# Mixing part of a two-layer encoder: decay chain and 16-block inverse on VectorE, rotary beside the root, two merges ahead of the last gate

## The chip, the cores and the metric

The kernel runs on one core of one Trainium2 chip. A core has five engines that follow their own instruction lists and wait for one another by semaphores: TensorE (PE, matmuls), VectorE (DVE), ScalarE (ACT), GpSimd (POOL) and SyncE (SP, which here only issues DMAs). The metric is device time in microseconds (us) of one execution of the whole program. An instruction list is executed in its order: an instruction that waits holds up everything behind it on its engine.

## The reference

`x` has 256 tokens of 1024 channels. After a first LayerNorm come two equal layers. Each is a mixing part and an expert part, each with a residual and a LayerNorm:

```python
p = h @ w_in            # 5648 columns, split by meaning:
ya = _global_gqa(aq, ak, av, ...)          # A: 8 query heads, 2 key heads, RMSNorm + rotary on q and k
yb = _neighbourhood_attn(bq, bk, bv, rpb)  # B: 4 heads, a window on the token grid
yc = _gdn_bidir(cq, ck, cv, cz, cbf, cbb, caf, cab, ...)  # C: gated delta rule, both directions
ga, gb, gc = sigmoid(gate logits)
mix = ga * (ya @ wa) + gb * (yb @ wb) + gc * (yc @ wc)
return mix @ w_out
```

Branch C is the long one. Its log decay is `g = -exp(A_log) * softplus(a + dt_bias)`; a five-tap convolution with SiLU makes q, k and v; q and k are scaled to unit length; and for each chunk of 64 tokens (4 chunks, 4 heads, 2 directions) a unit lower triangular 64 x 64 system is solved:

```python
decay = exp(where(incl, gc[..., :, None] - gc[..., None, :], -inf))   # gc: running sum of g
m   = where(strict, einsum('nbhid,nbhjd->nbhij', k_beta, kc) * decay, 0.0)
sol = triangular_solve(m + eye(C), rhs, lower=True, unit_diagonal=True)
```

The expert part routes each token to 2 of 32 SwiGLU experts; the weights of all 32 are read in each layer.

## The kernel before

Everything is kept in float32; the projections are made as three products of a high and a low part (`mm3`). Weights come in units of 128 x 1024 numbers. For each unit SP issues one DMA (`w_...`), ACT makes the high part (`uh_...`, a cast) and DVE the low part (`ul_...`, a subtraction, L190). The table `POOL` names the units whose low part POOL makes. The units stand in rings of four, so a DMA, a cast or a subtraction can only go ahead as far as products before it have been done.

TensorE's order is written out: `projections` goes through `ORDER`, the list of projections (`ga0`: first half of branch A's gate, `cqk`, `cz`, `cv`: branch C, `akv`, `aq`: branch A, `bqk`, `bv`: branch B, and the other gates), then `merge` multiplies each branch's result by its matrix (tiles `y0a...`, `y0b...`, `y0c...` in layer 0), `turn_mix` transposes the sum (`tpm`), and `project` does `w_out`, the residual, the LayerNorm and the router. Between two product groups `pump` may let a side line take its next step: `key_line`, `query_line` (rotary of branch A), `delta_line` (branch C), `attention_line` and `router_line` are generators, and the table `LAGS` says how long after one step the next is due, on a clock that `mm` counts up from the sizes of the matmuls. So `LAGS` sets where in TensorE's list a side line's matmuls stand. On the other engines a scheduler orders the instructions by readiness and by priority (`high_priority`), but `issue_after` and `manual_schedule` can pin them.

Names in what follows, in the order in which they occur in a layer:

- `conv(i, b)`: the convolution, ten multiplies-and-adds on DVE for each of three pieces (piece 2 is v, bank `cv`), a tanh on ACT and one more DVE instruction. `norm_rope`: RMS (square on ACT, reduce and scale on DVE, power -1/2 on POOL, L243, in `rsqrt`), then normalise (DVE), rotary (two POOL multiplies, one DVE multiply, one DVE addition). `k` gives `kTA`, `q` gives `qA`, transposed to `qTA`.
- `delta_line`, decay: softplus by a short series, some 20 instructions on DVE in the tiles `gap` and `sb` (16 columns each), ending with `g`. Then `eb` (sums of g by matmul), `R` (three POOL multiplies, 128 x 512), `db` (three products of R with masks), their exponentials `E` on ACT.
- `delta_line`, unit length: transposes `qk`, squares, reduce, `rsqrt`, then `kh` and two `qd` for each token half (placeA, placeF), transposed to `kT` and `qdT`; `gr` is the gram of k with k and q; sixteen DVE multiplies put the decay on it, which gives `Z`.
- `delta_line`, inverse: the 16 x 16 diagonal blocks of Z are picked (`Zc`), sent through memory to another layout (`d1`, `Zd`), inverted by 30 small instructions (L165, 15 to 64 columns), sent back (`d2`, `Wc`), spread into `X` and `Y` (placeF), and TensorE's `T16`, `X16`, `Y16`, `T32` build the 64 x 64 inverses from them.
- `PLACES` tells which tiles share a stretch of memory (placeA ... placeX); when a place is free, the first weights of the expert part are fetched into it.

All tiles of both layers have the layer's number in their names; the rows of the profile leave buffer numbers out. The functions that the change touches, with the line numbers of the profile:

Of the kernel before, what the change touches and what calls it, by code (L numbers as in the profile page):

```python
# [10 lines left out]
F32 = mybir.dt.float32  # L11
# [4 lines left out]
OP = mybir.AluOpType  # L16
# [29 lines left out]
POOL = (1, 2, 5, 13, 14, 15, 17, 18, 21, 23, 50, 62)  # L46
LAGS = {
    "delta": [15.03, 1.23, 3.7, 10.0, 0, 0.76, 53.51, 0, 0, 0.8, 0.24, 0.0, 0.52, 1.67, 1.37, 0, 2.87, 2.23, 0, 2.03, 1.99, 0, 2.87, 1.99, 0, 2.87, 6.3],
    "key": [10.0],
    "query": [16.22, 1.92, 1.92],  # L50
    "attention": [0, 6.46, 2, 0, 6.46, 1.24, 0, 6.46, 2, 0, 6.91, 2, 0, 6.46, 2, 0, 6.46, 2],
    "router": [7.35],
}
ORDER = ("ga0", "cqk", "cz", "cv", "akv", "aq", "ga1", "bqk", "bv", "gb0", "gb1", "gc0", "gc1")
# [63 lines left out]
def kernel(ctx: ExitStack, tc: tile.TileContext, a: dict, out: bass.AP):  # L118
# [24 lines left out]
    def st(shape, tag, name, bufs=1, dt=F32, side="left"):  # L143
# [134 lines left out]
    def stream(srcs, first, beside):  # L278
# [11 lines left out]
        def cut():  # L290
# [27 lines left out]
    def mixer(l, fetch, norm):  # L318
# [41 lines left out]
        for n in ORDER:  # L360
            if n[0] == "g":
                want(n, 2576 + "abc".index(n[1]) * 1024 + int(n[2]) * 512, 512)
            else:
                want(n, *COLS[n])
        NK = {"a": 4, "b": 2, "c": 2}
        for br in "abc":
            wv = a[f"w_branch_{br}"][l].rearrange("(k p) f -> p k f", p=128)
            w = 1024 // NK[br]
            for u in range(NK[br]):
                srcs.append((wv[:, :, u * w:(u + 1) * w], f"br{l}{br}{u}"))  # L370
        wo = a["w_out"][l]
# [180 lines left out]
        cs = [of(f"cs{i}", 2, S) for i in range(3)]  # L552

        def conv(i, b):
# [15 lines left out]
        def norm_rope(b, t, n, which, dst, name):  # L570
# [3 lines left out]
            xv = x8(x[:, :n * 64])  # L574
            raw = x8(b) if which else xv
            if not which:
                A.copy(x[:, :n * 64], b)
            sq = y
            A.activation(sq[:, :n * 64], b if which else x[:, :n * 64], AF.Square)
            rs = of(f"rs{t}", 8)  # L580
            V.tensor_reduce(out=rs[:, :n], in_=x8(sq[:, :n * 64]), axis=AX.X, op=OP.add)
            rsqrt(rs[:, :n], rs[:, :n], 1.0 / 64.0, 1e-6, n)
            tt(V, xv, raw, rs[:, :n, None].to_broadcast([128, n, 64]), OP.mult)
            yv = x8(y[:, :n * 64])
            s5 = gc_[:, which, 1, t].rearrange("p (a b e) -> p a b e", a=2, b=2)
            for b_ in range(2):
# [38 lines left out]
        def delta_line(vbank, zb):  # L625

            szg = of("szg", 2, 256)
            ba = of("ba", 2, 2, 2, 4)
            for t in range(2):
                V.tensor_copy(ba[:, :, :, t], zb[t][:, 256:272].rearrange("p (a d h) -> p a d h", a=2, d=2))  # L630
                A.activation(szg[:, t], zb[t][:, :256], AF.Tanh, scale=0.5)
                stt(szg[:, t], szg[:, t], 1.0, zb[t][:, :256], OP.add, OP.mult)
            tt(G, szg.rearrange("p t (h d) -> p (t h) d", d=64), szg.rearrange("p t (h d) -> p (t h) d", d=64),
               gn[:, 2:3].to_broadcast([128, 8, 64]), OP.mult)
            beta = of("beta", 2, 8)
            A.activation(beta, ba[:, 0].rearrange("p d t h -> p d (t h)"), AF.Tanh, scale=0.5)
# [1031 lines left out]
```

## Time and profile before

| | us |
|---|---|
| median of three runs | 1435.94 |
| lowest, highest | 1431.05, 1437.71 |
| the profiled execution | 1434.16 |
| its span, first to last instruction | 1432.4 |
| mixing part, layer 0 | about 0 to 270 |
| expert part, layer 0 | about 270 to 715 |
| mixing part, layer 1 | about 715 to 975 |
| expert part, layer 1 | about 975 to 1432 |

The limits between the parts are read from the timeline of TensorE. The profile shows one execution. A row of a timeline is one or several equal instructions in succession; "[3.64 <-DVE gap L169]" at its end says that the engine had stood idle 3.64 us before it and which instruction ended that. "PEclk 0.50" in a table of windows is TensorE's granted clock: 1.00 is 2.4 GHz, 0.50 is 1.2 GHz, and a value between them is a window with both.

### The profile page before, as it was taken

How to read it: one execution, taken by the hardware profiler on the slowest of the kernel's cores; microseconds unless marked ns; L12 is line 12 of the kernel's file. 1: busy time of each engine (PE TensorE's matmuls, PEld its weight loads, DVE VectorE, ACT ScalarE, POOL GpSimd, SP SyncE). 2: the span in 40 equal slices, each digit the busy share in tenths (PEclk: the TensorE clock that was granted, in tenths of full speed). 3: DMA queues.
4: the chain of work that ended last, by engine and by line, in shares of the span. 5: the costliest groups of instructions: out<-in, count | busy, mean ns of one | idle time of the engine just before them, and what ended most of it. 6: DMA issues, size and time to landing. Idle time of an engine off the chain costs nothing. (4 is left out here: it accounts for less than half of the span.)

```text
span 1432.4 us, 23895 instructions
## 1 busy us (share of the span) xinstructions
PE 1348.6 (94%) x9778; PEld 893.5 (62%) x9778; DVE 614.0 (43%) x1221; ACT 400.2 (28%) x761; POOL 258.6 (18%) x327
## 2 busy tenths in 40 slices
PE   8889999899998999999889999999999899999986
PEld 7877777655555555555377877875555555555632
DVE  6887567522231222222269866774222122222214
ACT  4445543211121111211144465332111111111111
POOL 4474303300000000000036661132000000000000
PEclk9989999999999999999999999999999999999998
DMA  7735769799999999999846366798999999999994
GB/s 231 213 107 145 245 243 347 303 408 418 419 418 414 419 419 418 419 418 420 350 142 205 122 194 223 269 354 314 420 419 419 418 419 418 418 419 419 418 419 194
DMA packets 114533, 479.88 MB, mean 335 GB/s; under 512 B 25169, under 2 KB 38001, under 8 KB 65521
## 3 DMA queue, kind: packets, MB, share of 16 engines
q1 hardware_dynamic: 112464, 471.85, 84.3%
q0 software_dynamic: 1376, 5.24, 1.0%
q8 instruction: 80, 1.31, 0.4%
q10 hardware_dynamic: 576, 1.18, 0.2%
q14 instruction: 37, 0.30, 0.1%
HBM read 476.40 MB, written 1.84 MB: 334 GB/s over the span
## 5 line engine op out<-in xcount | busy, mean ns | idle before, releaser
L180 PE MATMUL h<-w,h 128*64 128x256 f32 x2016 | 232.2, 387 | 21.8 <-PEq L1413 11.1
L180 PEld LDWEIGHTS h<-w,h 128*64 128x64 f32 x2016 | 144.0, 139 | 101.0 <-issue 16.9
L174 DVE SCALAR_TENSOR_TENSOR hid<-gate,h 128x256 f32<-128x256 f32 x64 | 26.9, 421 | 404.9 <-ACT gate L1504 404.9
L174 DVE SCALAR_TENSOR_TENSOR op<-mo,rt,op 64x512 fp32r<-64x512 f32 x128 | 96.0, 750 | 221.1 <-ACT op L1535 220.2
L1535 ACT ACTIVATE op<-mo,rt 64x512 fp32r<-64x512 f32 x128 | 87.4, 683 | 310.6 <-PE mo L180 271.2
L180 PE MATMUL mo<-w,hidT 128*64 128x512 f32 x720 | 168.1, 595 | 3.5 <-DMA w<-in_w_dram 2.0
L165 POOL TENSOR_TENSOR W<-P,rt 128x128 f32<-128x128 f32 x64 | 24.3, 400 | 774.8 <-PE PT L186 700.3
L1504 ACT ACTIVATE gate<-h 128x256 f32<-128x256 f32 x64 | 24.6, 384 | 405.9 <-PE h L180 405.9
L180 PEld LDWEIGHTS mo<-w,hidT 128*64 128x64 f32 x720 | 51.3, 137 | 92.3 <-issue 80.8
L180 PE MATMUL h<-w,xg 128*64 128x256 f32 x864 | 96.9, 380 | 2.4 <-ACT h L1478 2.4
L180 PE MATMUL h<-wl,h 128*64 128x256 f32 x768 | 86.3, 381 | 2.2 <-ACT h L1478 1.5
L180 PEld LDWEIGHTS h<-w,xg 128*64 128x64 f32 x864 | 61.0, 137 | 34.3 <-ACT h L1478 3.9
L180 PEld LDWEIGHTS h<-wl,h 128*64 128x64 f32 x768 | 53.9, 137 | 30.6 <-ACT h L1478 2.4
L180 PE MATMUL mo<-wl,hidT 128*64 128x512 f32 x304 | 69.8, 596 | 0.9 <-DMA wl<-in_w_dram 0.9
L180 PE MATMUL my<-op,PT 128*128 128x512 f32 x256 | 69.3, 410 | 0.8 <-DVE op L174 0.6
L180 PEld LDWEIGHTS my<-op,PT 128*128 128x128 f32 x256 | 45.4, 188 | 23.9 <-issue 13.2
L180 PE MATMUL xg<-P,hh 128*128 128x256 f32 x256 | 54.8, 294 | 0.3 <-DVE P L165 0.3
L180 PEld LDWEIGHTS xg<-P,hh 128*128 128x128 f32 x256 | 39.1, 188 | 24.8 <-issue 24.6
L180 PE MATMUL h<-wl,xg 128*64 128x256 f32 x416 | 48.3, 382 | 5.1 <-DMA wl<-in_w_dram 3.4
L180 PE MATMUL xg<-P,hl 128*128 128x256 f32 x256 | 51.0, 281 | 0.0
L180 PEld LDWEIGHTS mo<-wl,hidT 128*64 128x64 f32 x304 | 20.7, 137 | 35.5 <-issue 30.7
L180 PEld LDWEIGHTS h<-wl,xg 128*64 128x64 f32 x416 | 28.6, 137 | 22.5 <-DMA wl<-in_w_dram 6.5
(459 smaller groups left out, 2455.7 us busy)
## 6 DMA issues: line engine op xcount, KB each, us to landing
w<-in_w_dram SPq DMA_DIRECT2D x268, 1024.0 KB, 19.9
wl<-in_w_dram SPq DMA_DIRECT2D x112, 1024.0 KB, 19.9
w_gb<-in_w_in_dram SPq DMA_DIRECT2D x16, 512.0 KB, 3.6
w_gc<-in_w_in_dram SPq DMA_DIRECT2D x16, 512.0 KB, 4.6
w_wo<-in_w_out_dram SPq DMA_DIRECT2D x16, 512.0 KB, 4.4
w_ga<-in_w_in_dram SPq DMA_DIRECT2D x14, 512.0 KB, 5.4
w_cqk<-in_w_in_dram SPq DMA_DIRECT2D x8, 512.0 KB, 3.4
w_aq<-in_w_in_dram SPq DMA_DIRECT2D x8, 512.0 KB, 4.3
```

The costliest lines, as they stand in the source:

```text
L165: return eng.tensor_tensor(out=o, in0=x, in1=y, op=op).ins
L174: return V.scalar_tensor_tensor(out=o, in0=x, scalar=s, in1=y, op0=op0, op1=op1)
L180: ins = T.matmul(o, l, r, start=start, stop=stop, skip_group_check=True).ins
L1504: A.activation(g, b[:, :256], AF.Tanh, scale=0.5)
L1535: A.activation(hi, src, AF.Copy, scale=w)
```

## The change

What it does, piece by piece:

1. Decay: the series keeps its small tiles in a PSUM bank, takes fewer instructions (factors are folded into `scalar_tensor_tensor`), has -exp(A_log) made by POOL, and the convolution of v is placed behind it (`issue_after(decayed)`).
2. The convolution's first multiply is on ACT instead of DVE. The exponentials of `eb` are made twice, one copy in PSUM.
3. `norm_rope`: the rotary works on the raw values, beside the root; the normalisation comes last. The scale-and-add ahead of the power moves from DVE to POOL there and for the unit length of k and q.
4. `kh`, `qd`, the masks `Em` and the betas come in another order: transposes of v first, masks (all four now on DVE), a step of the side line, then `kh` and `qd`, pinned behind the last low part (`issue_after(scope["cut"])`). `cs[0]` lies where `kq` needs it, so the POOL copy L763 goes.
5. Blocks: `Zc` is made by one multiply and three multiply-adds; the 30 instructions of the inverse move from POOL to DVE; `X` is spread by four ACT copies, `Y` by one DVE multiply, instead of sixteen POOL multiplies.
6. `ORDER` has the merges of branches a and b ahead of `gc1`, c behind it. The gated sums of b and c stand in PSUM, and all additions to `mix` are on DVE.
7. The softmax normalisation moves from DVE to ACT; `LAGS`, `POOL` and `PLACES` have other entries.

The core of the diff:

```diff
-POOL = (1, 2, 5, 13, 14, 15, 17, 18, 21, 23, 50, 62)
+POOL = (1, 2, 5, 13, 14, 15, 17, 18, 21, 23, 56, 62)
 LAGS = {
-    "delta": [15.03, 1.23, 3.7, 10.0, 0, 0.76, 53.51, 0, ...
+    "delta": [15.03, 1.23, 3.7, 4.5, 5.5, 0, 0.76, 12.0, 20.0, 0, ...
-ORDER = ("ga0", "cqk", "cz", "cv", "akv", "aq", "ga1", "bqk", "bv", "gb0", "gb1", "gc0", "gc1")
+ORDER = ("ga0", "cqk", "cz", "cv", "akv", "aq", "ga1", "bqk", "bv", "gb0", "gb1", "gc0", "a", "b", "gc1", "c")
...
-    def rsqrt(o, x, scale, eps, n):
+    def rsqrt(o, x, scale, eps, n, eng=V):
         with tc.high_priority(offset=PRI):
-            ts(V, o, x, scale, OP.mult, eps, OP.add)
+            ts(eng, o, x, scale, OP.mult, eps, OP.add)
             return G.tensor_tensor(out=o, in0=o, in1=mhalf[:, :n], op=OP.pow)
...
             for m in range(2):                      # conv
-                ts(V, y[:, m], bv[:, m], cw[:, ch, 2:3], OP.mult)
+                A.activation(y[:, m], bv[:, m], AF.Copy, scale=cw[:, ch, 2:3])
...
-            rsqrt(rs[:, :n], rs[:, :n], 1.0 / 64.0, 1e-6, n)      # norm_rope
-            tt(V, xv, raw, rs[:, :n, None].to_broadcast([128, n, 64]), OP.mult)
+            rsqrt(rs[:, :n], rs[:, :n], 1.0 / 64.0, 1e-6, n, G)
...
             tt(V, xv, xv, gc_[:, which, 0, t:t + 1].to_broadcast([128, n, 64]), OP.mult)
-            tt(V, dst, xv, yv, OP.add)
+            tt(V, xv, xv, yv, OP.add)
+            tt(V, dst, xv, rs[:, :n, None].to_broadcast([128, n, 64]), OP.mult)
...
+            for c2 in range(2):                     # delta_line
+                decayed = stt(sc[:, c2], acc, C("half")[:, c2:c2 + 1], nea, OP.mult, OP.mult).ins
...
-            conv(2, vbank)
+            with tc.issue_after(decayed):
+                conv(2, vbank)
...
+            with tc.issue_after(scope["cut"]):
+                for t, b in enumerate(tokens):
+                    tt(V, x4(kh[:, t]), x4(b[:, 256:512]), bc(rk[:, t, 4:8]), OP.mult)
...
-                tt(G, tv, Zd[:, j + 1:, j:j + 1].to_broadcast([128, n, m]),
-                   W0[:, j:j + 1, :m].to_broadcast([128, n, m]), OP.mult)
-                tt(G, W0[:, j + 1:, :m], W0[:, j + 1:, :m], tv, OP.subtract)
+                    tt(V, tv, Zd[:, j + 1:, j:j + 1].to_broadcast([128, n, m]),
+                       W0[:, j:j + 1, :m].to_broadcast([128, n, m]), OP.mult)
+                    tt(V, W0[:, j + 1:, :m], W0[:, j + 1:, :m], tv, OP.subtract)
...
-            for w, o in ((1, Y), (0, X)):
-                for x0 in (0, 8):
-                    for b_ in range(4):
-                        tt(G, o[:, x0:x0 + 8, b_ * 16:b_ * 16 + 16], Wc[:, w, x0:x0 + 8],
-                           bm[:, b_:b_ + 1].to_broadcast([128, 8, 16]), OP.mult)
+            for b_ in range(4):
+                A.activation(X[:, :, b_ * 16:b_ * 16 + 16], Wc[:, 0], AF.Copy, scale=bm[:, b_, 0:1])
+            tt(V, Y.rearrange("p x (b j) -> p x b j", b=4), Wc[:, 1][:, :, None, :].to_broadcast([128, 16, 4, 16]),
+               bm[:, None].to_broadcast([128, 16, 4, 16]), OP.mult)
...
-                    stt(x, x, 1.0, b, OP.add, OP.mult)            # merge
-                    if br != "a":
-                        tt(G if br == "b" or t else V, mix[:, t, sl], mix[:, t, sl], x, OP.add)
+                    if br == "a":
+                        stt(x, x, 1.0, b, OP.add, OP.mult)
+                    else:
+                        with tc.high_priority(offset=PRI):
+                            stt(b, x, 1.0, b, OP.add, OP.mult)
+                            tt(V, mix[:, t, sl], mix[:, t, sl], b, OP.add)
```

How it moves instructions, at three places. First ACT in layer 0, where the exponentials of `eb` and `db` stand. Before:

```order
L190 CAST uh_ga101_787<-w_ga101_749 128x1024
L566 ACTIVATE cv0_513<-placeA0_99 128x512
L601 COPY placeJ0_104<-akv0_586 128x128
L579 ACTIVATE placeH0_105<-akv0_586 128x128
L190 CAST uh_ga102_867<-w_ga102_767 128x1024
L603 COPY placeG0_106<-placeG0_106 128x2x64
L690 ACTIVATE gap0_83<-eb0_797 128x64
L708 ACTIVATE placeB0_98<-db00_817 128x512
L603 COPY placeG0_106<-placeG0_106 128x2x64
L708 ACTIVATE placeB0_98<-db01_820 128x512
L708 ACTIVATE placeF0_103<-db02_823 128x512
```

and now:

```order
L605 COPY placeJ0_104<-akv0_586 128x128
L581 COPY placeH0_105<-akv0_586 128x128
L582 ACTIVATE placeG0_106<-akv0_586 128x2x64
L190 CAST uh_ga102_863<-w_ga102_771 128x1024
L572 ACTIVATE cv0_513<-placeA0_99 128x512
L691 ACTIVATE eb0_801<-eb0_801 128x64
L692 ACTIVATE gap0_83<-eb0_801 128x64
L710 ACTIVATE placeB0_98<-db00_820 128x512
L710 ACTIVATE placeB0_98<-db01_823 128x512
L607 COPY placeG0_106<-placeG0_106 128x2x64
L710 ACTIVATE placeF0_103<-db02_826 128x512
```

The tanh of the convolution of v (`cv`) stood five instructions ahead of the first exponential; it now stands directly ahead of it, and behind one more cast.

Second DVE in layer 0, where `kh` is made (placeA from `qk00` and `qk01`). Before:

```order
L171 TENSOR_SCALAR placeS0_108<-placeS0_108 128x8
L190 TENSOR_TENSOR ul_ga103_906<-w_ga103_785,uh_ga103_905 128x1024
L171 TENSOR_SCALAR placeS0_108<-placeS0_108 128x8
L165 TENSOR_TENSOR placeA0_99<-qk00_835,placeS0_108 128x256
L165 TENSOR_TENSOR placeF0_103<-qk00_835,gap0_83 128x256 x2
L190 TENSOR_TENSOR ul_bqk00_944<-w_bqk00_865,uh_bqk00_943 128x1024
L165 TENSOR_TENSOR placeA0_99<-qk01_847,placeS0_108 128x256
```

and now, from the last instruction of the rotary (placeE) on:

```order
L165 TENSOR_TENSOR placeE0_101<-placeH0_105,placeS0_108 128x512
L165 TENSOR_TENSOR placeI0_107<-placeI0_107,placeS0_108 64x256 x2
L190 TENSOR_TENSOR ul_bqk02_989<-w_bqk02_935,uh_bqk02_988 128x1024
L165 TENSOR_TENSOR placeI0_107<-placeI0_107,placeS0_108 64x256
L165 TENSOR_TENSOR placeF0_103<-placeF0_103,placeK0_109 128x512
L165 TENSOR_TENSOR placeB0_98<-placeB0_98,placeS0_108 128x512
L190 TENSOR_TENSOR ul_bqk03_1025<-w_bqk03_962,uh_bqk03_1024 128x1024
L165 TENSOR_TENSOR placeF0_103<-placeF0_103,placeS0_108 128x512 x2
L190 TENSOR_TENSOR ul_bv00_1125<-w_bv00_986,uh_bv00_1124 128x512
L165 TENSOR_TENSOR placeA0_99<-qk00_835,placeS0_108 128x256
L165 TENSOR_TENSOR placeF0_103<-qk00_835,gap0_83 128x256 x2
L165 TENSOR_TENSOR placeA0_99<-qk01_844,placeS0_108 128x256
```

`kh` stood ahead of the rotary's end and of the low parts of `bqk`; it now stands behind both, and behind the first low part of `bv`.

Third POOL in layer 0, between the rotary of q (placeH, 128x16x16) and the `kd` products (placeD). Now:

```order
L165 TENSOR_TENSOR placeH0_105<-placeH0_105,placeA0_99 128x16x16 x2
L171 TENSOR_SCALAR placeS0_108<-placeS0_108 128x8
L243 TENSOR_TENSOR placeS0_108<-placeS0_108,mhalf_64 128x8
L165 TENSOR_TENSOR placeH0_105<-placeH0_105,placeA0_99 128x16x16 x2
L171 TENSOR_SCALAR placeS0_108<-placeS0_108 128x8
L243 TENSOR_TENSOR placeS0_108<-placeS0_108,mhalf_64 128x8
L171 TENSOR_SCALAR placeS0_108<-placeS0_108 128x8
L243 TENSOR_TENSOR placeS0_108<-placeS0_108,mhalf_64 128x8
L171 TENSOR_SCALAR placeS0_108<-placeS0_108 128x8
L243 TENSOR_TENSOR placeS0_108<-placeS0_108,mhalf_64 128x8
L165 TENSOR_TENSOR placeD0_102<-placeA0_99,placeS0_108 128x512 x2
```

Before, three powers stood ahead of the first rotary and one between the two rotaries; now the first rotary comes first, and the power of q's second half (the last of the four) stands behind all the others.

## Rows read from the trace of the kernel before

**Rows 1.** Windows in layer 0: length, busy us (count) per engine, PEclk, DMA share, GB/s.

```profile
74.00:76.00 2.00, 2.00 (x4) 0.70 (x3) 1.95 (x10) 0.60 (x1) 1.76 (x4) 0.50 0.06 22
270.00:280.00 10.00, 9.53 (x81) 6.61 (x81) 3.46 (x12) 1.39 (x4) 1.67 (x5) 1.00 0.53 178
290.00:700.00 410.00, 392.57 (x2827) 226.28 (x2824) 96.81 (x189) 70.82 (x149) 10.61 (x28) 0.99 1.01 418
```

**Rows 2.** Waits of TensorE by what was waited for, layer 0; total, times, longest.

```profile
PE eb L180 <- DVE gap L169: 3.6, 1, 3.6
PE qTA L186 <- DVE placeE L165: 3.5, 1, 3.5
PE tpm L186 <- DVE mix L165: 0.9, 1, 0.9
...
PE qTA L186 <- ACT placeI L771: 0.8, 1, 0.8
PE tpm L186 <- POOL mix L165: 0.7, 1, 0.7
```

**Rows 3.** The same view, layer 1.

```profile
PE eb L180 <- DVE gap L169: 2.9, 1, 2.9
PE qTA L186 <- DVE placeE L165: 2.6, 1, 2.6
```

**Rows 4.** Timeline of TensorE, layer 0; start, us, work [idle before].

```profile
71.46 1.97 PE L180 MATMUL eb<-gap,placeK 128*128 128x8 f32 x12 [3.64 <-DVE gap L169]
...
76.56 1.02 PE L180 MATMUL db<-placeC,placeK 128*128 128x512 f32 x2
...
80.64 0.39 PE L180 MATMUL ga<-uh_ga,placeT 128*128 128x512 f32 x1
...
94.90 0.60 PE L186 MATMUL kT<-cst,placeA 128*128 128x128 f32 x4
...
102.39 0.90 PE L186 MATMUL qTA<-cst,placeE 128*128 128x128 f32 x3 [3.53 <-DVE placeE L165]
...
105.78 1.67 PE L180 MATMUL gr<-placeD 64*64 64x128 f32 x32
...
156.12 1.15 PE L180 MATMUL T<-placeF,placeA 64*64 64x64 f32 x32
```

**Rows 5.** Timeline of GpSimd, layer 0.

```profile
61.60 2.40 POOL L190 TENSOR_TENSOR ul_aq<-w_aq,uh_aq 128x1024 fp32r<-128x1024 f32 x1 [1.65 <-ACT uh_aq L190]
...
67.47 1.52 POOL L165 TENSOR_TENSOR placeH<-placeH,placeA 128x64 f32<-128x64 f32 x2 [2.63 <-DVE sb L174]
71.48 1.04 POOL L165 TENSOR_TENSOR placeG<-gap,placeK 128x512 f32<-128x512 f32 x1 [2.48 <-DVE gap L169]
...
83.43 6.47 POOL L243 TENSOR_TENSOR placeS<-placeS,mhalf 128x8 f32<-128x8 f32 x3
...
96.29 2.72 POOL L165 TENSOR_TENSOR placeH<-placeH,placeA 128x256 f32<-128x256 f32 x2 [0.87 <-DVE placeH L165]
...
122.34 0.51 POOL L165 TENSOR_TENSOR placeJ<-placeJ,placeB 128x15 f32<-128x15 f32 x1 [9.89 <-DMA placeJ<-d]
...
144.00 9.77 POOL L165 TENSOR_TENSOR placeF<-placeC,placeK 128x128 f32<-128x128 f32 x16 [4.42 <-DMA placeC<-d]
```

**Rows 6.** Timeline of VectorE, layer 0.

```profile
61.90 0.16 DVE L169 TENSOR_SCALAR sb<-gap 128x16 f32<-128x16 f32 x1
...
62.28 1.75 DVE L171 TENSOR_SCALAR placeS<-placeS 128x2 f32<-128x2 f32 x1
63.94 0.47 DVE L174 SCALAR_TENSOR_TENSOR placeA<-cv,placeS,placeA 128x254 f32<-128x254 f32 x1
...
65.36 1.22 DVE L190 TENSOR_TENSOR ul_ga<-w_ga,uh_ga 128x1024 fp32r<-128x1024 f32 x1
...
114.16 1.97 DVE L798 TENSOR_REDUCE placeJ<-placeB 128x256 f32<-128x1024 f32 x1
```

**Rows 7.** Timeline of ScalarE, layer 0.

```profile
67.08 0.60 ACT L566 ACTIVATE cv<-placeA 128x512 f32<-128x512 f32 x1 [2.21 <-DVE placeA L174]
```

More of the change, by code (lines that the diff above doesn't have):

```diff
@@ L297, in cut @@
                 made = split(u[0], u[1], w, G if i in POOL else V)
+            if i not in POOL:
+                scope["cut"] = made[1]
             ready.append(u)
@@ L551, in mixer @@
         kd, kq, qT = (of(n, 2, 2, S) for n in ("kd", "kq", "qT"))
-        cs = [of(f"cs{i}", 2, S) for i in range(3)]
+        cs = [kq[:, 1]] + [of(f"cs{i}", 2, S) for i in (1, 2)]
         def conv(i, b):
@@ L627, in delta_line @@
             szg = of("szg", 2, 256)
[L628 to L634, printed above, removed]
+            sb = bank("s", f"sb{l}")
+            rr, sq_, acc, th_ = (sb[:, 16 * i:16 * i + 16] for i in range(4))
+            by_t = lambda ap: ap.rearrange("p (d t h) -> p d t h", d=2, t=2)
+            by_d = lambda ap: ap.rearrange("p (d h) -> p d h", d=2)
             beta = of("beta", 2, 8)
-            A.activation(beta, ba[:, 0].rearrange("p d t h -> p d (t h)"), AF.Tanh, scale=0.5)
-            ts(V, beta, beta, 0.5, OP.mult, 0.5, OP.add)
             sc = of("gsc", 8, 16)
-            av = ba[:, 1].rearrange("p d t h -> p (d t h)")
+            xx, ax, ee, ss, pp, g = (sc[:, i] for i in range(6))
             ea = of("ea", 8)
@@ L642, in delta_line @@
                 A.activation(ea, al[:, 0], AF.Exp)
-            def dh(ap8):
-                return ap8.rearrange("p (d h) -> p d h", d=2)[:, :, None, :].to_broadcast([128, 2, 2, 4])
-            xx, ax, ee, ss, pp, g = (sc[:, i] for i in range(6))
-            sb = bank("s", f"sb{l}")
-            rr, sq_, acc = (sb[:, 16 * i:16 * i + 16] for i in range(3))
-            tt(V, xx.rearrange("p (d t h) -> p d t h", d=2, t=2), ba[:, 1], dh(al[:, 1]), OP.add)
+            nea = sc[:, 6]
+            for t in range(2):
+                ts(G, by_t(nea)[:, :, t], by_d(ea), -1.0, OP.mult)
+            for t in range(2):
+                tt(V, by_t(xx)[:, :, t], by_d(zb[t][:, 264:272]), by_d(al[:, 1]), OP.add)
+            for t in range(2):
+                A.activation(by_t(th_)[:, :, t], by_d(zb[t][:, 256:264]), AF.Tanh, scale=0.5)
+                A.activation(szg[:, t], zb[t][:, :256], AF.Tanh, scale=0.5)
+                stt(szg[:, t], szg[:, t], 1.0, zb[t][:, :256], OP.add, OP.mult)
             stt(ax, xx, -1.0, xx, OP.mult, OP.max)
@@ L994, in softmax @@
             for t in range(2):
-                ts(V, pr[:, t], pr[:, t], mx[:, 2 + t:3 + t], OP.mult)
+                A.activation(pr[:, t], pr[:, t], AF.Copy, scale=mx[:, 2 + t:3 + t])
             return pr
@@ L1093, in projections @@
                     spawn("delta", delta_line(vbank, zb))
+                elif len(n) == 1:
+                    if n != "a":
+                        wait({"b": "attention", "c": "delta"}[n])
+                    if n == "c":
+                        wait("router")
+                        free("T", "U")
+                    yield from merge(n)
                 elif n == "akv":
@@ L1249, in mixer @@
             pump()
-        wait("attention")
-        wait("router")
-        free("T", "U")
-        for br in "abc":
-            if br == "c":
-                wait("delta")
-            for _ in merge(br):
-                pump()
         for _ in project():
```

107 lines of the change are left out of this document (56 added, 51 removed), and 2 rows, old and new, of the table PLACES.

## The prediction

> **What bounds the kernel now.** I read the windows first. In the expert part of layer 0 the DMA engines are busy all the time (share 1.01, 418 GB/s), so that part takes as long as its weights take [rows 1]. At its beginning, 270 to 280 us, they are only half busy (0.53, 178 GB/s): the weights that could be fetched early have been, and the rest waits for buffers that the experts themselves free. So the end of the mixing part moves the end of the layer one for one, both ways. Then the list of what TensorE waited for, in the mixing part: TensorE is the engine whose list sets the end there, and what can be won or lost is its waits and the time at the low clock after them. In layer 0 they are 3.6 us before `eb` (for the decay chain on DVE), 0.8 and 3.5 us before `qTA` (for the rotary), 0.9 and 0.7 us before the first `tpm` (for the gated sums) [rows 2]; in layer 1 they are 2.9 and 2.6 us and the same tail [rows 3]. The timeline shows the places: `eb` at 71.46, `ga1` at 80.64, `kT` at 94.90, `qTA` at 102.39, `gr` from 105.78 to 107.45, `T16` at 156.12 with no wait ahead of it [rows 4]. After a wait of this length the granted clock is 0.50, that is 1.2 GHz: 74 to 76 us shows it [rows 1].
>
> **The decay chain.** Its some 20 small instructions and g now stand ahead of the convolution of v, so `eb` can follow the last product of `aq` at once, at 71.46 - 3.64 = 67.8. That removes 3.6 us (layer 1: 2.9). What is late next is the third `db`. Its bank comes free when ACT has read the first `db`; ACT stands in order behind the tanh of the convolution of v (first order fences). That tanh needs the last multiply-add of the convolution; DVE stands in order behind the sum of k's rotary, and that behind POOL. POOL's walk in layer 0, by rows 5: low part of `aq` from 61.60 to 64.0; two `R` at 1.04, 66.1; a small scale, 0.3 (estimate, between 0.16 on DVE [rows 6] and 0.51 for POOL's 15 columns); third `R`, 67.4; the power of two columns, 0.6 (a fourth of 6.47 / 3 = 2.16, rounded up); the two rotary multiplies, 1.52: 69.5. DVE then has five multiply-adds at 0.4 (0.47 less the overlap), two low parts at 1.15 (1.22 less the overlap) and three small ones at 0.2 [rows 6]: 4.9, so 74.4. Tanh 0.6 [rows 7], two small exponentials some 0.4, the exponential of the first `db` 0.6 like the tanh: 76.0. TensorE is there at about 70.7 (`eb` and two `db` took 76.56 - 71.46 = 5.1 us mostly at the low clock, so some 2.9 at the full one). The wait is thus not gone but moved by a few lines: 5.3 us instead of 3.6. From the third `db` to `ga1` it took 4.1 us (80.64 - 76.56); this stretch is now the one at the low clock, some 6. `ga1` begins at about 82 instead of 80.64: +1.4.
>
> **Rotary and unit length.** `qTA` no longer waits: it stands behind `kT`. But `kT` needs `kh`, which in DVE's order now stands behind the last instruction of q's rotary, and this behind the fourth power on POOL (second and third fences). The walk: `aq`'s first half is done at 76.0 + 3.0 = 79.0 (third `db` and three products at the low clock), copied at 79.6; on POOL rotary 2.7, scale and power 2.46, rotary 2.7, three times scale and power 7.4 [rows 5]: 94.9. On DVE then: the rotary's last multiply 0.6, three half-height multiplies at 0.4, two low parts 2.3, four multiplies of 512 columns at 0.6 (half a low part), a half low part 0.6: 7.1, and `kh` 0.4: 102.4. TensorE comes to `kT` 94.90 - 80.64 = 14.3 after `ga1`, at 96.3: a wait of 6.1, where `qTA` had 4.3. And more stands behind it: before, `qTA`, twelve products of `bqk` and `gr` followed (107.45 - 102.39 = 5.1); now `kT`, twelve of `bqk`, `qdT`, `qTA`, twelve more, `gr`. `kT`'s second half needs another four DVE instructions (0.5 beyond `kT`'s own first half); `kT` 0.6, the products 2.8 at the low clock, `qdT` and `qTA` 2.3, then 1.7 and 1.0 for the rest as the clock comes back: 8.9. `gr` ends at 111.3 instead of 107.45: +3.9, in which the +1.4 is contained. In layer 1 TensorE waited 2.4 us less before (5.5 against 7.9 [rows 2, 3]) and nothing in the walk is shorter by as much, so there it is +5 or so.
>
> These are the durations next to busy neighbours. The rotary multiplies are the uncertain ones: 1.52 and 2.72 a pair where DVE was at work. At best a multiply of 256 columns takes what the 512 of `R` allow, half of 1.04; then two pairs of q and the pair of k take 3.7 us less, and layer 0 comes to about 0, layer 1 to +1. From above: if the four multiplies of 512 columns on DVE meet POOL and take half as long again, +1.2 each layer. I take a point nearer to the rows: +3 and +4.
>
> What the page GPSIMD Engine Reference of the Trainium skill says (section Key points) bears on this: GpSimd shares its memory interfaces with VectorE and contends with DVE instructions that run in a two-port mode or have two inputs in SBUF. The trace agrees: the small scale on DVE took 1.75 us while POOL made a low part, and one that writes to PSUM took 0.16 in the same stretch [rows 6]. By that rule the rotary would run free, since DVE mostly waits beside it, and the sum would be near the lower end; it is the second rival.
>
> **Blocks.** `gr` to `Zc` becomes shorter: the reduce of 1.97 [rows 6] and the multiply before it (1.2, like a low part) go, four instructions of 256 columns come (0.4 each): -1.6, and as the list is otherwise shorter there, up to -3.7. The inverse on POOL lasted from 122.34 to 137.8, that is 144.00 - 4.42 = 139.6 less the copy and the issue of the DMA. On DVE 30 dependent instructions take 30 x 0.2 = 6.2, but they stand among five low parts (5.7) and reduces of `s_a` (some 2.5): about 14, hardly shorter. The sixteen multiplies on POOL, 9.77 [rows 5], become one of 1.2 on DVE. So X and Y are ready about 13 us earlier (153.8 before). But `T16` stands about 18 us earlier in TensorE's list than 156.12, some 138.3, with `gr`'s shift on both sides. TensorE waits about 1 us (from 0 to 4) where it did not wait. Nothing is won by the earlier place: between `bv` and the merges TensorE had no wait of size. +1 a layer.
>
> **Tail.** The gated sums of b and c need no POOL; its 0.7 goes. The 0.9 remains in part, since the first of the new instructions stands on DVE behind two low parts of `w_out`. -0.7 a layer. Beside these I cost at nothing: the softmax normalisation on ACT and the convolution's multiplies on ACT (ACT is idle half of the mixing part; if ACT were late there, `cv` would be late too, within the walk above), the masks on DVE (in the walk), the other places of tiles.
>
> **Sum.** 3 + 4 + 2 - 1.4 = +7.6 on the profiled execution's 1434.2: 1441.8. That execution lies 1.8 us below the median, within the runs' spread; I predict 1441.
>
> **The rivals.**
> 1. Both waits only trade places (25 in 100). POOL's rotary runs free, the clock falls less, `T16` is on time: 0 + 1 + 0 - 1.4, about 1434. For it: 2.72 for a pair beside a busy DVE against 1.04 for a whole `R`. Against it: the powers, 6.47 for three, are as long without any neighbour, and four of them stand in a row.
> 2. The change does what it looks like (15 in 100). `db` and `kT` find their inputs in time, as they would if k's rotary on POOL ended before `aq`'s last products, and q's powers before `bqk`. Then 7.9 and 5.5 us go, some 4 and 3 us of low clock too, less about 2 a layer that is built in: `kh` stands behind the low part of `bv`'s first unit, whose cast waits for the 24th product of `bqk` itself (0.6 + 0.6 + 0.4). 1434 - 16.4 - 1.4, about 1416; halfway, 1425.
> 3. Slower by DVE's load (18 in 100). The 30 small instructions are each held by low parts that wait for casts, and casts wait for TensorE's products: a chain through three engines. If the inverse ends 5 us later than I summed, TensorE waits 5 to 6 us at `T16`, falls to the low clock and loses about 2 us more: +6 a layer on top, about 1452. [...] Against it: the low parts ahead of `T16` are made from units that are there already.
>
> **How the numbers follow.** My forecast has 42 in 100, for 1436 to 1446. What a measurement of this kernel can tell from no change is about 0.5%, 7.2 us: faster is below 1428.8, slower above 1443.1. Faster holds the second rival and a little of the first, 0.18; slower the third and the upper part of mine, 0.37; the rest, 0.45, is within 0.5%. The range leaves out the good half of rival 2 and the worst of rival 3: 1427 to 1452.
>
> **What would show it.** Right: no wait at `eb`, but one of 4 to 6 us at the third `db` in both layers, behind the tanh of `cv`; none at `qTA`, but one of 4 to 7 at `kT`; `gr` 2 to 5 us later; a wait of 0 to 4 at `T16`; one instead of two waits at `tpm`. Wrong: `db` without a wait (then POOL was early), `kT` with under 2 us, or a `T16` above 4 us. That DMA is half idle at the beginning of the expert part must stay; if its share there were near 1, the mixing part's end would no longer count in full.

## The result, and the profile after

| us | before | after |
|---|---|---|
| median | 1434.33 | 1468.59 |
| lowest, highest | 1431.05, 1437.71 | 1463.88, 1472.4 |
| profiled execution | 1434.16 | 1463.88 |
| its span | 1432.4 | 1462.1 |

The ratio is 1.024 with an interval of [1.022, 1.0261]: slower by 34 us, where 7 were forecast. The profiled execution is the shortest of the four after, so 4.5 us of the difference of the medians can't be read from it; between the two profiles lie 29.7. Nothing of it arises in the expert parts. There the DMA engines still are half busy at the start, 10 us behind the router, as in [rows 1] (a window of after; columns as there):

```profile
284.00:294.00 10.00, 9.56 (x80) 6.89 (x80) 4.21 (x12) 1.39 (x4) 2.40 (x5) 1.00 0.47 155
```

So the time is lost in the two mixing parts, and TensorE's waits there show where. First layer 0 (0 to 280 us; total, times, longest), which answers to [rows 2]:

```profile
PE kT L186 <- DVE placeA L165: 6.7, 2, 6.2
PE db L180 <- ACT placeB L710: 5.2, 1, 5.2
PE T L180 <- DVE placeF L165: 4.2, 1, 4.2
PE vn L180 <- ACT placeF L889: 2.5, 1, 2.5
...
PE ob L180 <- ACT placeJ L932: 2.0, 1, 2.0
...
PE gb L180 <- ACT gb L1137: 1.1, 1, 1.1
```

and layer 1 (700 to 1010 us), which answers to [rows 3]:

```profile
PE kT L186 <- DVE placeA L165: 6.6, 2, 6.1
PE T L180 <- DVE placeF L165: 4.3, 1, 4.3
PE db L180 <- ACT placeB L710: 4.0, 1, 4.0
PE vn L180 <- ACT placeF L889: 2.5, 1, 2.5
PE ob L180 <- ACT placeJ L932: 2.0, 1, 2.0
```

`eb` and `qTA` are gone from the list. In their place stand `db` and `kT`, as forecast, and then four entries that were not there before: `T16` of 4.2, and three of ACT's (`vn`, `ob`, `gb`) that together make 5.7. TensorE's timeline in layer 0, to be laid beside [rows 4]:

```profile
76.19 2.04 PE L180 MATMUL db<-placeC,placeK 128*128 128x512 f32 x2 [5.24 <-ACT placeB L710]
...
81.91 0.48 PE L180 MATMUL ga<-uh_ga,placeT 128*128 128x512 f32 x1
...
102.69 0.45 PE L186 MATMUL kT<-cst,placeA 128*128 128x128 f32 x1 [6.24 <-DVE placeA L165]
...
110.28 1.10 PE L180 MATMUL gr<-placeD 64*64 64x128 f32 x32
...
147.20 1.97 PE L180 MATMUL T<-placeF,placeA 64*64 64x64 f32 x32 [4.24 <-DVE placeF L165]
...
174.30 0.68 PE L180 MATMUL vn<-placeI,placeF 64*64 64x64 f32 x14 [2.52 <-ACT placeF L889]
...
273.82 0.41 PE L180 MATMUL lg<-gap 128*128 128x32 f32 x2
```

`lg`, the router's product (its first half), stood here before:

```profile
259.05 0.41 PE L180 MATMUL lg<-gap 128*128 128x32 f32 x2
```

So layer 0 is 14.8 us late at its router. Up to the end of `gr` it is 3.9 (111.38 against 107.45). From the end of `bv` to `lg` the waits grow from 3.4 to 11.1, which is 7.7, and TensorE's own work takes 3.2 longer. Most of the 3.2, some 2.6, is the low clock in one stretch behind the wait at `T16` (the last window below; busy time times the share of the clock that is missing, an estimate); before, the clock stood at 1.00 all the way from `bv` to `lg`. The first two windows show the same behind the waits at `db` and `kT`; they lie ahead of the end of `gr`, in the stretch where before it was low behind `eb` and `qTA`. PEclk is third from the end:

```profile
74.00:80.00 6.00, 3.81 (x7) 2.42 (x8) 5.79 (x20) 3.21 (x8) 1.59 (x3) 0.50 0.79 256
...
102.00:108.00 6.00, 4.85 (x22) 4.59 (x23) 3.65 (x9) 0.64 (x2) 2.04 (x2) 0.50 0.38 121
...
146.00:152.00 6.00, 4.80 (x41) 3.79 (x43) 1.05 (x1) 2.02 (x5) 0.00 (x0) 0.50 0.38 143
```

3.9 + 7.7 + 3.2 = 14.8. Layer 1 is 16.2 late by the same count, from its own start. The expert part of layer 0 gives 1.7 back, that of layer 1 takes 0.4: 14.8 - 1.7 + 16.2 + 0.4 = 29.7.

Why `T16` is late, on DVE (the inverse's first and last instruction, and `Y`):

```profile
122.95 0.17 DVE L165 TENSOR_TENSOR placeJ<-placeJ,placeB 128x15 f32<-128x15 f32 x1
...
137.14 0.17 DVE L165 TENSOR_TENSOR placeB<-placeB,placeJ 128x15 f32<-128x15 f32 x1
...
145.83 1.22 DVE L165 TENSOR_TENSOR placeF<-placeC,placeK 128x1024 f32<-128x1024 f32 x1 [2.58 <-DMA placeC<-d]
```

The inverse takes 14.4 us, since its 0.2 us instructions stand among low parts of 1.22. `T16` takes `Y` alone. `Y` is ready at 147.05. Before, `X` was done at 153.8, but `Y`'s eight multiplies came first, so `Y` was there at some 148.9 (half of the row of 9.77 in [rows 5], an estimate). So `Y` is some 2 us earlier, while TensorE asks for it at 142.96, 13 earlier. And why `vn` is late, on ACT, whose last copy (L889) frees TensorE:

```profile
170.49 0.91 ACT L1004 ACTIVATE placeH<-placeH,placeS 128x256 f32<-128x256 f32 x2
171.57 1.04 ACT L190 CAST uh_gc<-w_gc 128x1024 fp32r<-128x1024 f32 x1 [0.17 <-PE gb L180]
172.52 0.47 ACT L1001 ACTIVATE placeH<-s_a,placeS 128x256 f32<-128x256 f32 x1
...
173.87 0.38 ACT L889 ACTIVATE placeF<-L 32x256 f32<-32x256 f32 x1
```

L1004 is the softmax normalisation that moved from DVE. ACT hardly waits here (0.17 us); it does one thing after the other.

### The profile page after: what moved, and what is told of

Same layout as the page of the kernel before. It is cut to its first block, busy times and chain, and to the rows that moved or that the text cites. A ratio compares the mean times of both kernels' runs of the same rounds, so it can differ in the third digit from the quotient of the medians.

```text
span 1462.1 us, 23868 instructions
## 1 busy us (share of the span) xinstructions
PE 1355.9 (93%) x9778; PEld 899.6 (62%) x9778; DVE 597.0 (41%) x1227; ACT 429.1 (29%) x839; POOL 178.0 (12%) x229
## 3 DMA queue, kind: packets, MB, share of 16 engines
q0 software_dynamic: 1376, 5.24, 1.0%
## 5 line engine op out<-in xcount | busy, mean ns | idle before, releaser
L180 PEld LDWEIGHTS my<-op,PT 128*128 128x128 f32 x256 | 45.4, 188 | 23.9 <-issue 13.2
```

The lines of the kernel that those rows point to most:

```text
L180: ins = T.matmul(o, l, r, start=start, stop=stop, skip_group_check=True).ins
```

## The experiments

All are compared with the kernel before, which ran beside them (medians 1433.2 to 1434.8). "The first repair" is `kh` early, "the second" the lag of 27, "the third" the normalisation on POOL.

| kernel | median | ratio | interval |
|---|---|---|---|
| after | 1468.59 | 1.024 | 1.022 to 1.0261 |
| e1_kh (first repair) | 1457.05 | 1.0153 | 1.0133 to 1.0173 |
| e2_lag (second) | 1456.20 | 1.015 | 1.0134 to 1.0167 |
| e3_softmax | 1474.33 | 1.0281 | 1.0263 to 1.0298 |
| e4_exps | 1467.41 | 1.0222 | 1.0202 to 1.0241 |
| e5_khlag (first and second) | 1441.63 | 1.0062 | 1.0046 to 1.0077 |
| e9_khlag41 | 1452.28 | 1.0134 | 1.0116 to 1.0152 |
| e7_pool | 1485.27 | 1.0358 | 1.0337 to 1.0379 |
| e6_tail (on the kernel before) | 1446.04 | 1.0088 | 1.0073 to 1.0103 |
| e10_smpool (all three) | 1434.22 | 1.0005 | 0.9994 to 1.0017 |
| e11_notail | 1447.53 | 1.0101 | 1.008 to 1.0122 |
| e12_both | 1441.99 | 1.0061 | 1.0045 to 1.0078 |
| e15_lag24 | 1441.33 | 1.0048 | 1.0033 to 1.0063 |
| e13_krv | 1429.72 | 0.9972 | 0.996 to 0.9985 |
| e14_nodec | 1430.03 | 0.9968 | 0.9957 to 0.9979 |
| e17_nodeconly | 1467.13 | 1.0227 | 1.0211 to 1.0244 |
| e16_nodeckrv | 1428.18 | 0.996 | 0.9945 to 0.9976 |

**e1_kh.** `kh` and `qd` right behind the root, as before the change:

```diff
                 rsqrt(rk[:, t], rk[:, t], 1.0, 1e-6, 8, G)
-                tokens.append(b)
+                tt(V, x4(kh[:, t]), x4(b[:, 256:512]), bc(rk[:, t, 4:8]), OP.mult)
...
-            with tc.issue_after(scope["cut"]):
-                for t, b in enumerate(tokens):
```

> The changed kernel with one thing undone: kh and qd are made right behind the root of k and q, as before, and not behind the masks and the low parts. Main theory (each wait has its own displaced instruction, and costs its length plus the low clock behind it): kT's wait of 6.2 + 0.45 us per layer falls to under 1.5, because the third power on POOL ended at 92.8 and TensorE comes to kT at 96.4; gr ends 5 to 8 us earlier; 13 to 18 us of the whole, so 1451 to 1456. Rival (the wait is the visible end of a chain; another wait comes in its place, at qTA or gr): less than 7 us, over 1461.

1457.05, between the two. The wait at `kT` is gone and `gr` ends 8.2 us earlier, but layer 0's router is only 2.4 earlier. What stands behind gave it back:

```profile
PE db L180 <- ACT placeB L710: 5.4, 1, 5.4
PE T L180 <- DVE placeF L165: 4.3, 1, 4.3
PE vn L180 <- ACT placeF L885: 2.5, 1, 2.5
PE ob L180 <- ACT placeJ L928: 2.0, 1, 2.0
```

`T16` waits as long as ever: its place in the list moves with `gr`, and so do its inputs. Of the 5.8 us that are lost again, 1.6 lie between `gr` and the end of `bv`, 1.3 are longer waits behind it, and some 3 are the clock: the waits at `vn` and `ob` are as long as in the kernel after, where the clock stayed at 1.00 behind both, but here it fell behind both (windows, columns as above):

```profile
170.00:174.00 4.00, 4.00 (x30) 3.00 (x30) 1.78 (x8) 0.30 (x2) 0.00 (x0) 0.57 0.35 123
...
208.00:212.00 4.00, 3.82 (x31) 3.70 (x32) 1.60 (x4) 0.73 (x2) 0.00 (x0) 0.57 0.89 317
```

**e2_lag.** Branch C's steps from `T16` on due seven units later on the clock of `LAGS`, which sets them some 5 us of products later in TensorE's list:

```diff
-    "delta": [15.03, 1.23, 3.7, 4.5, 5.5, 0, 0.76, 12.0, 20.0, 0, ...
+    "delta": [15.03, 1.23, 3.7, 4.5, 5.5, 0, 0.76, 12.0, 27.0, 0, ...
```

> The changed kernel with one number of LAGS changed: the step that holds T16 is due 27 instead of 20 after the one before it, so T16 and all that follows it in branch C stand later in TensorE's list by some 4 to 5 us of matmuls. Main theory: T16's wait of 4.2 us and the low clock behind it go, and vn's 2.5 shrinks or goes, since its inputs have more time; 10 to 16 us of the whole, 1452 to 1458. Rival (branch C is the long chain to the merge of c; a later T16 only moves its wait to the end): less than 4 us, 1465 to 1470.

1456.20, as the main theory had it. `T16`, `vn` and `ob` are no longer in the list of waits, and the largest new one is

```profile
PE kv L180 <- ACT placeJ L932: 1.6, 1, 1.6
```

So the early place of `T16` and of all that follows it costs some 12 us, with work unchanged.

**e3_softmax.** The normalisation back on DVE:

```diff
-                A.activation(pr[:, t], pr[:, t], AF.Copy, scale=mx[:, 2 + t:3 + t])
+                ts(V, pr[:, t], pr[:, t], mx[:, 2 + t:3 + t], OP.mult)
```

> The changed kernel with the softmax normalisation (two multiplies by a column, 256 wide, per score bank) back on DVE. Main theory: ACT, in order, had copies that TensorE needs (placeF of L32 for vn, the copy of vn for ob, the gate's bank) behind softmax work; with less of it vn's 2.5 and ob's 2.0 fall by at least half; 4 to 9 us of the whole, 1460 to 1465. Rival (DVE is the engine that is short, since the inverse is there): T16's wait of 4.2 grows by 1 or more, whole 1467 to 1474.

1474.33, the rival's side and just above its range: slower by 5.7. ACT's waits shrink, DVE's appear, though `T16`'s grows by 0.6 only:

```profile
PE T L180 <- DVE placeF L165: 4.8, 1, 4.8
PE ks L180 <- DVE placeS L174: 2.8, 2, 2.6
PE vn L180 <- ACT placeF L889: 1.7, 1, 1.7
```

**e4_exps.** The tanh of the convolution of v and its last DVE instruction behind the three exponentials of `db`:

```diff
-                conv(2, vbank)
+                gated = conv(2, vbank)
...
+            with tc.issue_after(last):
+                gated()
```

> The changed kernel with the tanh of the convolution of v, and the last multiply-add behind it, placed behind the three exponentials of db in ACT's order instead of ahead of them. Main theory: the third db no longer waits (5.2 us in layer 0, 4.0 in layer 1), ga1 begins 4 to 5 us earlier, and since POOL's chain for kT starts from aq, kT's wait keeps its length and gr moves with ga1; 8 to 13 us of the whole, 1456 to 1461. Rival (k's rotary on POOL and the low parts of ga1 on DVE are as late): a wait of 3 us or more at kTA or ga1 in its place, less than 4 us of the whole.

1467.41, the size that the rival gave, but not at its places (`kTA`, `ga1`): in layer 0 the wait at `db` goes from 5.2 to 4.0, and that at `kT` grows from 6.2 to 8.2, with `kT` itself at the same place (102.68 against 102.69).

**e5_khlag and e9_khlag41.** Both repairs at once; then the same with a lag of 41.5, `T16` about where it was before the change.

> The kernel after with both repairs at once: kh and qd right behind the root, and branch C's lag 27 instead of 20. Main theory (the time is the sum of TensorE's waits and of the low clock behind them; the wait at kT and the waits at T16, vn and ob are separate places): the two gains add up, 1468.6 - 11.5 - 12.4 = 1444.7, so 1442 to 1448; no wait of over 1 us at kT, T16, vn or ob. Rival (behind gr the chain over DVE, ACT and the DMA for the 16-blocks sets the pace; what is gained at gr is given back by new waits further on, as most of it was in layer 0 when only kh was moved): 1451 to 1456, with a wait of 2 us or more between bv and the merges.

> As the one before, with a lag of 41.5: T16 stands again where the kernel before had it in TensorE's list, in the middle of the first gate of c. Main theory (T16's inputs are there about 4 us after TensorE asks for them in the kernel after; any place some 7 us further on is late enough, and more brings nothing): 1442 to 1449, no wait at T16, the recurrence then ends beside the last merges and ycT waits 0 to 2 us. Rival (DVE and ACT are also the short engines there, and more room brings more): 1437 to 1441.

1441.63: the gains add up (11.5 + 12.4 = 23.9; measured 27.0). But 1452.28 for the later place: both theories were wrong there. Without a wait at `T16` the recurrence, now the last thing in the layer, waits itself, and the clock is low behind the first two of these waits (0.50 from 180 to 182 and from 218 to 220 us). Against e5_khlag the waits between `bv` and `lg` are 2.7 longer and the low clock takes some 1.7 more, of 5.3 that this stretch is longer:

```profile
PE L L180 <- ACT placeC L871: 2.6, 2, 2.2
...
PE ks L180 <- DVE placeS L174: 2.0, 1, 2.0
PE y0c L180 <- ACT ym L190: 1.7, 1, 1.7
```

**e7_pool.** The kernel after with the inverse and its transposed copy on POOL. The edit also takes away the pins that held the inverse's place (`high_priority`, `manual_schedule`, `issue_after`):

```diff
-                    tt(V, tv, Zd[:, j + 1:, j:j + 1]...
+                tt(G, tv, Zd[:, j + 1:, j:j + 1]...
```

> The kernel after with the 16-blocks' inverse (30 instructions and the transposed copy) back on POOL, everything else as in the kernel after. Main theory (it is not the engine: the inverse takes 15.4 us on POOL and 14.4 on DVE; T16 comes too early in TensorE's list): the wait at T16 stays at 4 to 7 us; DVE has 6 us less to do, which helps the casts a little; 1464 to 1472. Rival (the inverse on DVE is what is late, since it stands among casts): the wait at T16 goes below 2 us, 1458 to 1462.

1485.27, outside both. The inverse was not slower: it ended at 136.1 on POOL, against 137.3 on DVE. But ACT's list now has the first instruction of `X` ahead of casts and softmax copies, and it waits there for the DMA. ACT's row, and what TensorE then waits for instead of `T16`:

```profile
142.40 0.51 ACT L836 ACTIVATE placeF<-placeC,placeK 128x256 f32<-128x256 f32 x1 [14.07 <-DMA placeC<-d]
```

```profile
PE o_a L180 <- ACT placeH L1011: 13.1, 1, 13.1
```

So the run does not tell which engine is the better one for the inverse. It shows what `X` on ACT costs once it stands too early there: 16.7 us. Whether it was the engine or the missing pins that moved `X` was not tested.

**e6_tail, e11_notail.** The kernel before with the new `ORDER` and sums alone; and the kernel with two repairs with the old tail (the same lines turned round):

```diff
-ORDER = (..., "gc0", "gc1")
+ORDER = (..., "gc0", "a", "b", "gc1", "c")
...
+                            tt(V, mix[:, t, sl], mix[:, t, sl], b, OP.add)
```

> The kernel before with the tail of the change alone: the merges of a and b ahead of the last gate of c, the gated sums in the PSUM bank and on DVE. The waits at tpm are 0.93 + 0.74 us a layer before and 0.4 after. Main theory: 1.2 us a layer go, 1434.8 - 2.4 = 1432.4, so 1430.5 to 1433.5, below what can be told from no change. Rival (the reordered list also takes the low clock or other waits with it, such as those at the gates of c): 1425 to 1429. Other rival (the early merges want w_branch's weights earlier than the DMA or the casts have them): 1437 or more, with a wait at y0a.

> The kernel after with kh early and the lag of 27 (1441.6), but with the tail of the kernel before: the merges of a and b behind both gates of c, the sums outside PSUM, on DVE and POOL. Main theory (in the kernel before the new tail cost 11 to 13 us because its sums stand on DVE in front of the last step of branch C; with branch C as early as here that cost is not there, and the new tail saves its wait at tpm): slower than 1441.6 by 1 to 4, 1442 to 1446. Rival (the new tail costs here too): 1429 to 1437.

1446.04 and 1447.53. By itself the tail costs 12 us; in the kernel with two repairs it saves 5.9. In the first, branch C is still at work when the sums of b come, and these, with their high priority, stand on DVE in front of its last subtraction:

```profile
PE vn L180 <- DVE placeJ L165: 3.9, 1, 3.9
```

From `bv` to `lg` layer 0 takes 6.4 longer than before: 3.5 of waits, and some 2.9 of low clock behind this one (0.50 from 214 to 218 us). With branch C 13 us earlier (its last product ends at 203.9 in e5_khlag, at 217.1 here) it has ended by then, and only the gain at `tpm` is left: 0.4 a layer, against these two waits with the old tail:

```profile
PE tpm L186 <- DVE mix L165: 1.7, 1, 1.7
PE tpm L186 <- POOL mix L165: 1.6, 1, 1.6
```

The main theory had the second nearly right (1442 to 1446) and missed the first entirely; the other rival had the first's size, but the wait is not at `y0a`.

**e10_smpool, e12_both.** The normalisation on POOL (`ts(G, ...)` in the line of e3), with the two repairs; and that with the old tail.

> The kernel after with kh early and the lag of 27 (1441.6), and the softmax normalisation on POOL, which is nearly idle from 130 to 206 us. In the run with both repairs TensorE still waits for ACT at kv (1.5), L (1.2), gb (1.2), pT_a (1.0) and o_a (0.6) in a layer. Main theory (these waits come from ACT, which works its list in order and has too much in it): some 3 of the 5.5 us a layer go, 1434 to 1438. Rival (the wait only moves: the normalisation on POOL is slower than on ACT, 0.6 against 0.5, with one more hand-over, so pT waits for POOL): 1440 to 1446.

> As the one before, with the softmax normalisation on POOL too. If the two changes don't touch each other, the time is 1441.6 plus both differences; by the main theories of the two some 1437 to 1441, by both rivals 1429 to 1440.

1434.22, within the main theory's range, and 1441.99, just above all that was expected. The third repair brings 7.4 (5.5 with the old tail). With the three, the 34 us are gone: 11.5, 12.4, 3 for both together, 7.4. What then waits for POOL is 2.0 in layer 0 and 2.7 in layer 1, below what ACT had cost.

**e15_lag24.** The kernel with three repairs, with 24.0 instead of 27.0 in the line of e2.

> The kernel with the three repairs (1434.2), with branch C's lag at 24 instead of 27, between the change's 20 (wait of 4.2 us at T16) and 27 (none). If the lag's gain grows step by step with the place: 1437 to 1441, with a wait of 1 to 3 us at T16. If it is a matter of one place in the list (the second X16 or the recurrence against the softmax): 1431 to 1435.

1441.33, at the upper end of the first range. But `T16` waits 0 and 1.2 us only; `tpm` has 1.9 in each layer, behind the sums on DVE. The routers are 3.5 and 2.6 us late, and in layer 0 some 1.2 of this is a longer stretch of low clock ahead of `T16`. Three steps of lag cost 7 us and seven steps 12 (e2): it is no single wait that goes.

**e13_krv, e14_nodec.** With the three repairs TensorE still waits 4.8 and 5.5 us at the third `db`, and DVE has this row:

```profile
69.20 0.30 DVE L165 TENSOR_TENSOR akv<-akv,placeH 128x128 f32<-128x128 f32 x1 [5.99 <-POOL placeH L165]
```

One kernel makes k's rotary multiplies on DVE, the other no longer holds the convolution of v behind the decay chain:

```diff
-                tt(G, o, i0, i1, OP.mult)
+                tt(V if which else G, o, i0, i1, OP.mult)
```

```diff
-            with tc.issue_after(decayed):
-                conv(2, vbank)
+            conv(2, vbank)
```

> The kernel with the three repairs (kh early, lag 27, softmax normalisation on POOL; 1434.2), and k's rotary multiplies on DVE instead of POOL. There TensorE waits 4.8 (layer 0) and 5.5 us (layer 1) at the third db; DVE stands from 63.1 to 69.2 us before the last sum of k's rotary, since POOL makes its product at 68.56, behind a low part, two R, a scale, the third R and a power. Main theory (the wait at db is POOL's order carried on by DVE and ACT): the wait falls below 1.5 us and the low clock after it goes too, 4 to 6 us a layer, 1422 to 1427, faster than both kernels. Rival (the next product of DVE, the one by the power made on POOL at 67.87, holds the same chain; or DVE's four more instructions are late themselves): the wait stays above 3 us, 1430 to 1437.

> The kernel with the three repairs (1434.2), but the convolution of v not held behind the decay chain, so that its multiply-adds stand between the chain's instructions on DVE as they did in the kernel before. Theory A (the decay chain first is worth nothing, since the wait at eb only becomes one at the third db): eb waits 2 to 5 us and db below 2, 1431 to 1437. Theory B (it costs: db stands behind more of ACT's work than eb did): 1426 to 1430. Theory C (it gains): 1438 or more, with waits at both eb and db.

1429.72 and 1430.03, both faster than the kernel before by 4 us. The first lies between the ranges of its two theories, the second at the edge of theory B. With k's rotary on DVE the wait is halved, to

```profile
PE db L180 <- DVE placeC L174: 2.4, 1, 2.4
```

Without the hold there is no wait at `eb` and none at `db`, where I had expected one of the two; `qTA` waits instead:

```profile
PE qTA L186 <- DVE placeE L165: 2.7, 1, 2.7
```

So the decay chain's new place was a loss of 4.2 us behind the repairs.

**e17_nodeconly, e16_nodeckrv.** The hold taken out of the kernel after alone; and both edits with the three repairs.

> The kernel after, with only the hold of the convolution of v behind the decay chain taken out. The wait at db is 5.2 and 4.0 us there, and behind the three repairs its loss was worth 4.2. If the parts of the loss stay separate: 1463 to 1466, no wait at eb or db. If the wait at kT takes what is won, as it did when only the exponentials were moved ahead of the tanh (1467.4): 1466.5 to 1470, with a wait at kT of 9 us or more.

> The kernel with the three repairs, the convolution of v not held behind the decay chain (1430.0), and k's rotary multiplies on DVE as well (alone 1429.7 from 1434.2). Theory A (both edits remove the same wait at the third db, so they don't add): 1429 to 1432. Theory B (k's rotary on DVE also frees POOL for q's, whose wait at qTA is 2.7 us a layer when the convolution is not held): 1423 to 1427.

1467.13, as the second theory had it, and 1428.18, between the two. In the first the wait at `db` goes and nearly all of it comes back at `kT`, whose own chain is no earlier:

```profile
PE kT L186 <- DVE placeA L165: 11.6, 2, 10.5
```

The second is the fastest of these kernels, 0.4% below the kernel before. The two edits remove in part the same wait: 4.5 and 4.2 alone, 6.0 together.

## Why the prediction was wrong

- **What bounds the kernel**: right. The delay at the end of the mixing part passes through the expert part, 13.1 of 14.8 us.
- **Decay chain**: right, number by number (`db` at 76.19 after 5.24 us for 76.0 and 5.3, `ga1` at 81.91 for about 82). What it hangs on was right too: DVE in order behind k's rotary, that behind POOL (e13_krv). There is some luck in the number: on POOL the low part of `aq` began 0.9 us later than in the rows, and the rotary's two multiplies took 0.60 where 1.52 was set, so the two errors cancel.
- **Rotary and unit length**: the walk was right (`kT` 102.69 for 102.4, `gr` 111.38 for 111.3); the step that failed is taking "a point nearer to the rows", +3 and +4, for +3.9 and +5.1. The reason for it came true, q's multiplies took 1.4 and 1.6 instead of 2.72, and yet nothing came of it: POOL's small scales took up to 1.2 where 0.3 was set, and the last power ended at 94.78 for 94.9. (The case in which the rotary runs free is called the second rival there; in the list it is the first.) What spoke against that rival did not hold: a power took 1.64 beside an idle DVE and up to 2.52 beside a busy one.
- **Blocks**: here the prediction failed, at "+1 a layer". Its own two numbers, 140.8 for X and Y and 138.3 for the place of `T16`, leave 2.5; the value taken was below them. Measured are 4.2, as Y came 2.3 us later behind `gr` than summed. The inverse was on time; all of the 2.3 is its way through memory, which the sum took over as it was before: from its end to the start of `Y` it is 8.5 us (137.3 to 145.83), before 6.2 (137.8 to 144.00 in [rows 5]). Some 1.3 of that is the write `d2` (DMA issues of after and of before; the last column is us from issue to landing):

```profile
d<-placeB POOLq DMA_DIRECT2D x2, 128.0 KB, 3.4
```

```profile
d<-placeB POOLq DMA_DIRECT2D x2, 128.0 KB, 2.1
```

  The clock was left out, though rival 3 had it: 4.8 us of work at 0.50 after the wait is some 2.4 us lost. e2_lag shows what the place costs with all that stands behind it: 12.4 us. "Nothing is won by the earlier place" was right; that something is lost by it was not seen.
- **"Beside these I cost at nothing"**: failed, for the normalisation on ACT. "ACT is idle half of the mixing part" is an average; where `vn` and `ob` want ACT's copies, casts, exponentials and normalisations stand in front of them. ACT's three waits are 5.7 us a layer, and behind the other two repairs the normalisation on POOL instead of ACT brings 7.4 in all (e10_smpool). That is not the price of the move from DVE: taken back alone it made the kernel slower (e3_softmax). And with `T16` later (e2_lag) the copies for `vn` and `ob` were in time, so these waits hang on the place of branch C as well.
- **Tail**: `tpm` went from 1.7 to 0.4, so -1.25 for -0.7, but e6_tail shows that the sign hangs on branch C's place.
- **Sum and rivals**: 2 us of the error are the shading at `gr`, nearly all the rest is the two steps above: in layer 0, 5.6 at `T16` (4.2 and 2.4, less the 1 forecast) and 5.7 at ACT's three waits. Rival 3 had the mechanism, a late `T16` with the low clock behind it, and at 1452 half of its size, as it ended at `T16` and did not follow the list on to `vn` and `ob`. DVE's load, its name, was not the cause: the inverse took the 14 us summed for it.

The Trainium skill's GPSIMD Engine Reference (section Key points) was set against the trace at the rotary, where its rule was to bring the sum near the lower end. The trace agrees with the rule, as q's multiplies took 1.42 and 1.57 beside a DVE that mostly stood or made reduces, which have one input (2.72 in [rows 5], beside a low part and a sum, which have two), but the end of the chain did not move with them.

What stays open: which engine should do the inverse, why the clock falls behind a wait in one kernel and not behind an equal one in another, and what the new entries of `POOL` and `PLACES` and `X` on ACT are worth alone, which no run tests.

## What to carry to other kernels

When an edit moves a long side line earlier in the list of the engine that sets the end, walk every later step of it, not its first: each takes its inputs from engines that had slack only because the step stood late. "Idle half of the time" is not a price; look at what stands in front of the one instruction that TensorE will wait for. Waits in a row hide one another (the hold taken out gave 1.5 us, no more than the uncertainty, and 4.2 behind the repairs), so a change whose parts cost should be taken apart from its last wait back as well as from its first on.

## What was not expected of the hardware

Contention between POOL and DVE reaches small instructions, and both ways. In e13_krv a multiply of 64 columns on DVE took 2.05 us beside a POOL low part of 2.40, and two of them 0.35 when POOL was idle:

```profile
62.97 2.05 DVE L165 TENSOR_TENSOR placeH<-placeH,placeA 128x64 f32<-128x64 f32 x1
...
73.48 0.35 DVE L165 TENSOR_TENSOR placeH<-placeH,placeA 128x64 f32<-128x64 f32 x2
```

and in e7_pool POOL's instructions of 28 columns, one beside a low part on DVE and one not:

```profile
123.29 1.24 POOL L165 TENSOR_TENSOR placeJ<-placeJ,placeB 128x28 f32<-128x28 f32 x1
124.61 0.24 POOL L165 TENSOR_TENSOR placeB<-placeB,placeJ 128x28 f32<-128x28 f32 x1
```

TensorE's granted clock was 0.50 (1.2 GHz) behind each of the three long waits of layer 0 (5.24, 6.24, 4.24 us), as the windows above show, and not behind that of 2.52 us at `vn` (window of after, columns as above):

```profile
174.00:178.00 4.00, 3.70 (x45) 2.90 (x46) 1.76 (x8) 1.69 (x5) 0.00 (x0) 1.00 0.62 230
```

But the length of a wait does not settle it. In e1_kh the wait at `vn` is 2.52 too, and the clock fell behind it (0.57 in the window of 170 to 174 us above). In e10_smpool it fell behind three short waits for POOL at `pT` (0.56, 0.86 and 0.57 us, from 134.6 to 137.5), between which TensorE had little to do (2.0 us of work from 134 to 138):

```profile
138.00:140.00 2.00, 2.00 (x7) 1.61 (x6) 0.24 (x1) 1.45 (x4) 0.00 (x0) 0.50 0.94 148
```

So a wait costs its length, and whether it costs a slow stretch as well is read from the windows behind it.
